# Short-convolution layer on one core: the weight sums of w_out made in the two-tile stage and kept in HBM, 15 seven-product pairs in place of 10

## The chip, the core and the metric

One NeuronCore of a Trainium2 chip. TensorE (PE) multiplies, with its weight loads (PEld) beside it; VectorE (DVE) and ScalarE (ACT) work on elements; GpSimd (POOL) does some adds and issues DMAs of its own; SyncE (SP) issues nearly all other DMAs. The metric is device time of one execution, in microseconds (us), median over runs; lower is better.

## What is computed

One layer of a decoder trunk for 256 tokens of width D = 2048, with E = 4096 channels, all in float32:

```python
h = rmsnorm(x, norm_g)
shift, scale, gate = split(silu(c) @ ada_w + ada_b, 3)
h = h * (1 + scale) + shift
b_gate, c_gate, v, g = split(h @ w_in, 4)          # w_in is D x 4E
u = causal_depthwise_conv(c_gate * v, conv_w)      # width 3
y = b_gate * u * silu(g)
x = x + gate * (y @ w_out)                         # w_out is E x D
return rmsnorm(x, final_g)
```

## The kernel before

Every float32 product is done as three products of reduced parts (`triple`): with a = a_hi + a_lo, the terms are hi*hi, hi*lo and lo*hi. So each weight tile is loaded by DMA, its high part is cast on ScalarE (line 380, and 842), and its low part, the difference, is made on VectorE (line 385, and 845). Weight tiles are 128 x 2048 (1 MB) in a pool `wpool` with three places of each kind, used in turn: "raw", "hi" and "lo".

The program has three stages. In the first (tiles `mm_s`) 16 of the 32 channel tiles are projected while the modulation is still being summed. In the **two-tile stage** (tiles `mm_b`, loop `for ct in range(NS, NCT, 2)`) the other 16 are projected two at a time: for each pair of channel tiles four quarters of w_in, and for each quarter two steps of one weight tile with 48 matmuls of 128x256. That makes 64 steps. After each step `gate_piece` adds a part of the sums for the gate: a load `at_g` and two multiply-adds on VectorE, 32 pieces in all, in four column groups. When a group is complete, GpSimd folds its 128 partitions in seven rounds (two copying DMAs into `turned` and an add each, lines 708 to 710), and adds it to the gate's bias (line 712), which SP has loaded onto all partitions (line 673).

In the **w_out stage** y is multiplied by w_out in two passes: first columns 0 to 1023, then 1024 to 2047 (of which the last 512 are partly done in a closing part with the channels in `LAST`). A pass (`columns`) goes over *pairs* of channel tiles in a written order; a pair is 256 rows of w_out. A plain pair needs eight triples, 24 matmuls of 128x512. A pair in `SEVEN` is done by a Strassen-Winograd scheme on 2x2 blocks with seven triples, 21 matmuls. It needs sums of the pair's four weight blocks b0 to b3, which `seven` makes on VectorE (lines 837, 843, 844), and sums of the tokens, made for each such pair in the two-tile stage by `token_forms` and kept in SBUF (`form`). Pairs 10 to 15 are of that kind in the first pass, 10 to 13 in the second, and a plain pair mostly stands between two of them.

In this stage "lo" places hold what is loaded or summed (`raw_o`, `sums_o`), "raw" places hold low parts and "hi" places high parts. A place is given out in turn, so a tile waits for the last reader of the tile three places earlier. Each engine runs its instructions in the order in which the program's scheduler wrote them; SP too, so a DMA whose place is not free holds up the ones behind it. The order on an engine is the scheduler's unless a manual dependency sets it, such as `last_low`, which keeps pairs in sequence on VectorE.

Of the kernel before, what the change touches and what calls it, by code (L numbers as in the profile page):

```python
# [8 lines left out]
F32 = mybir.dt.float32  # L9
# [108 lines left out]
def short_conv_layer(ctx: ExitStack, tc: tile.TileContext, x, c, norm_g, ada_w, ada_b, w_in, conv_w, w_out, final_g, out):  # L118
# [551 lines left out]
    gates = [slot([P, 2, 512], f"gate{j}") for j in range(2)]  # L670
    zs = [slot([P, 2, 2, T], f"z{j}") for j in range(2)]
    for j in range(2):
        nc.sync.dma_start(
            gates[j].rearrange("p a f -> p (a f)"),
            ada_b[0:1, 2 * D + j * 1024 : 2 * D + (j + 1) * 1024].partition_broadcast(P),
        )

    def gate(dc):
        return gates[dc // 2][:, dc % 2, :]
# [14 lines left out]
    def gate_sums(dc, j, at3):  # L694
# [10 lines left out]
        if j + 2 == KT:  # L705
# [6 lines left out]
            nc.gpsimd.tensor_tensor(out=gate(dc), in0=ga, in1=gate(dc), op=ALU.add)  # L712
# [3 lines left out]
    SEVEN = range(10, 16)  # L716
# [3 lines left out]
    def token_forms(pair, u):  # L720
# [9 lines left out]
        if pair < 14:  # L730
# [9 lines left out]
        nc.vector.tensor_tensor(out=lo, in0=sums, in1=hi.bitcast(F32), op=ALU.subtract)  # L740

    for ct in range(NS, NCT, 2):
        for q in QUARTERS:
            bank = psum.tile([P, CT, T], F32, tag="mm", name="mm_b")[:, 0:2]
            col = q * E + ct * P
            for kp in range(0, KT, KP):
# [12 lines left out]
                gate_piece()  # L759
            z = zs[q // 2][:, q % 2]  # L760
# [20 lines left out]
    W = 512  # L781
# [6 lines left out]
    def load_ends(n):  # L788

        if 0 <= n < TT:  # L790
            nc.sync.dma_start(xr[:, n, :], x[n * P : (n + 1) * P, :])
        elif n == TT:
            nc.sync.dma_start(fg, final_g.rearrange("(o d) -> o d", o=1).partition_broadcast(P))

# [6 lines left out]

    def load_o(raw, e0, ne, c0, n):
        nc.sync.dma_start(
            raw.rearrange("p (k f) -> p k f", k=ne),
            w_out[0, e0 * P : (e0 + ne) * P, c0 : c0 + n].rearrange("(k p) f -> p k f", p=P),
        )
# [9 lines left out]
    def residual(t, c0, n, src, pr):  # L816
# [3 lines left out]
        g = gates[c0 // 1024].rearrange("p a f -> p (a f)")[:, c0 % 1024 : c0 % 1024 + n]  # L820
        nc.vector.tensor_tensor(out=pr, in0=src, in1=g, op=ALU.mult)
# [9 lines left out]
    def seven(j, raw, bank, p1, p6, p75, opens, last):  # L831


        sums = w_tile("lo", "sums_o")
        hi, lo = hi_tile(), lo_tile("raw")
        b, s, bh, bl = (v.rearrange("p (b f) -> p b f", f=W) for v in (raw, sums, hi, lo))
        first = nc.vector.tensor_tensor(
            out=s[:, 0:2], in0=b[:, 1:3], in1=b[:, 0:1].to_broadcast([P, 2, W]), op=ALU.subtract
        )
        if last_low[0] is not None:  # L840
            tc.add_manual_dep(first.ins, last_low[0].ins.name, after, reason="the pair in front comes first")
        nc.scalar.copy(bh[:, 1:4], b[:, 1:4])
# [178 lines left out]
```

## Time and profile before

| | |
|---|---|
| median of 3 runs | 901.03 us (900.9 to 901.96) |
| span of the profiled execution | 898.9 us |
| what lies around the span, from the median | 2.1 us |
| VectorE busy in the span | 75% |
| ScalarE busy in the span | 54% |
| DMA moved | 235.53 MB, mean 262 GB/s |

The span is the time from the first to the last instruction of one execution. The page gives the busy share of each engine, the chain of work that ended last (followed back from the last instruction to what released each), the groups of instructions with their mean duration, the idle time in front of them and what ended it, and the DMA issues with the time to landing. A row of windows gives for each stretch the busy us of PE, PEld, DVE, ACT and POOL with their instruction counts, then the granted clock, the busy share of the DMA engines and GB/s.

### The profile page before, as it was taken

Reading aid. Unit: us, or ns where it says so; the run is one execution under the profiler, and the core shown is the slowest. Engines: PE = TensorE matmul, PEld = TensorE weight load, DVE = VectorE, ACT = ScalarE, POOL = GpSimd, SP = SyncE. Lnnn points to the kernel's source line nnn. Section 1 sums busy time; section 2 is a strip of 40 time slices with the busy share of each in tenths; the row PEclk is TensorE's granted clock in tenths of the full one; section 3 lists DMA queues with packets and bytes.
Section 4 is the critical chain, followed back from the end, with each engine's and each line's share of the span. In section 5 each row is a group of like instructions: output and inputs, shape, how many; then the busy total and the mean of one; then the engine's idle time right before and its main releaser. Section 6 shows DMA issues by size and latency. Waiting matters only on the chain.

```text
span 898.9 us, 16428 instructions
## 1 busy us (share of the span) xinstructions
PE 886.5 (99%) x6989; PEld 849.7 (95%) x6989; DVE 674.4 (75%) x667; ACT 484.0 (54%) x430; POOL 95.6 (11%) x107
## 2 busy tenths in 40 slices
PE   7999999999999999999999999999999999999996
PEld 4999999999999999999999999999999988888885
DVE  5899988899888866755965677565555578879896
ACT  6768866665558856644433444443434445554543
POOL 0000001010000134024134103410000000000000
PEclk9999999999999999999999999999999999999998
DMA  9999999999998597687888789766666476674662
GB/s 309 369 369 368 369 336 361 347 365 367 372 318 291 167 277 231 196 266 244 278 246 242 252 273 274 233 207 204 193 188 188 141 290 224 192 276 126 202 234 94
DMA packets 160250, 235.53 MB, mean 262 GB/s; under 512 B 7028, under 2 KB 105924, under 8 KB 159792
## 3 DMA queue, kind: packets, MB, share of 16 engines
q1 hardware_dynamic: 156368, 226.52, 76.8%
q0 software_dynamic: 3680, 7.92, 3.2%
q8 instruction: 55, 0.90, 0.4%
q14 instruction: 19, 0.16, 0.0%
q10 hardware_dynamic: 128, 0.04, 0.0%
HBM read 224.49 MB, written 2.10 MB: 252 GB/s over the span
## 4 chain that ended last, share of the span: by engine, by line
PE 97%; DMA 2%; SPq 0%; ACT 0%; issue 0%; ACTq 0%; DVE 0%
PE mm_s L545 39%; PE mm_b L545 39%; PE mm_w L814 7%; PE mm_o L814 7%; PE mm L814 4%; DMA at<-in_ada_w_dram 2%; PE sum L418 0%; SPq L240 0%; PE tp_g L530 0%; PE tp_g L526 0%; ACT big L928 0%; ACTq L1017 0%; ACT fs L918 0%; ACT z L991 0%; DVE fs L919 0%
## 5 line engine op out<-in xcount | busy, mean ns | idle before, releaser
L545 PE MATMUL mm_b<-hT,hi 128*128 128x256 f32 x2048 | 348.2, 276 | 0.0
L545 PE MATMUL mm_s<-hT,hi 128*128 128x256 f32 x2048 | 335.6, 277 | 0.0
L545 PEld LDWEIGHTS mm_b<-hT,hi 128*128 128x128 f32 x2048 | 308.1, 188 | 0.0
L545 PEld LDWEIGHTS mm_s<-hT,hi 128*128 128x128 f32 x2048 | 299.0, 188 | 0.2
L545 PE MATMUL mm_b<-hT,lo 128*128 128x256 f32 x1024 | 282.6, 276 | 0.0
L545 PE MATMUL mm_s<-hT,lo 128*128 128x256 f32 x1024 | 261.3, 276 | 0.0
L385 DVE TENSOR_TENSOR lo<-raw,hi 128x2048 fp32r<-128x2048 f32 (+1 forms) x66 | 152.4, 2311 | 103.1 <-ACT hi L380 102.6
L380 ACT CAST hi<-raw 128x2048 fp32r<-128x2048 f32 (+1 forms) x66 | 123.7, 1874 | 192.7 <-PE mm_b L545 146.6
L545 PEld LDWEIGHTS mm_b<-hT,lo 128*128 128x128 f32 x1024 | 192.2, 188 | 0.0
L545 PEld LDWEIGHTS mm_s<-hT,lo 128*128 128x128 f32 x1024 | 182.4, 188 | 0.0
L385 DVE TENSOR_TENSOR lo<-raw_s,hi 128x2048 fp32r<-128x2048 f32 (+1 forms) x80 | 149.1, 1871 | 34.7 <-ACT hi L380 34.2
L380 ACT CAST hi<-raw_s 128x2048 fp32r<-128x2048 f32 (+2 forms) x81 | 124.1, 1541 | 61.7 <-PE mm_s L545 46.7
L515 DVE SCALAR_TENSOR_TENSOR gv<-at,silu_c,gv 128x512 f32<-128x512 f32 x105 | 79.0, 752 | 5.5 <-DMA at<-in_ada_w_dram 3.6
L568 ACT COPY acc<-mm_s 128x1024 f32<-128x1024 f32 x54 | 54.6, 1012 | 37.0 <-PE mm_s L545 37.0
L385 DVE TENSOR_TENSOR lo<-raw_o,hi 128x2048 fp32r<-128x2048 f32 x22 | 50.4, 2290 | 22.9 <-ACT hi L380 22.9
L380 ACT CAST hi<-raw_o 128x2048 fp32r<-128x2048 f32 x22 | 42.0, 1908 | 45.8 <-DMA raw_o<-in_sc_w_out_dram 12.3
L814 PE MATMUL mm_w<-hi,y 128*128 128x512 f32 x184 | 58.8, 389 | 0.0
L710 POOL TENSOR_TENSOR gacc<-gacc,z 128x512 f32<-128x512 f32 x28 | 45.6, 1628 | 106.8 <-DMA z<-gacc 106.8
L814 PE MATMUL mm_o<-hi,y 128*128 128x512 f32 x176 | 55.3, 389 | 0.0
L704 DVE SCALAR_TENSOR_TENSOR gacc<-at_g,silu_c,gacc 128x512 f32<-128x512 f32 x60 | 46.9, 782 | 6.0 <-DMA at_g<-in_ada_w_dram 4.8
L814 PEld LDWEIGHTS mm_w<-hi,y 128*128 128x128 f32 x184 | 34.5, 188 | 7.2
L582 ACT COPY mm_s<-acc 128x1024 f32<-128x1024 f32 x38 | 38.6, 1017 | 2.6 <-DVE acc L571 1.8
(161 smaller groups left out, 670.8 us busy)
## 6 DMA issues: line engine op xcount, KB each, us to landing
raw<-in_sc_w_in_dram SPq DMA_DIRECT2D x64, 1024.0 KB, 5.8
raw_s<-in_sc_w_in_dram SPq DMA_DIRECT2D x47, 1024.0 KB, 7.9
raw_o<-in_sc_w_out_dram SPq DMA_DIRECT2D x32, 1024.0 KB, 5.2
at<-in_ada_w_dram SPq DMA_DIRECT2D x126, 256.0 KB, 7.8
raw_s<-in_sc_w_in_dram SPq DMA_DIRECT2D x33, 512.0 KB, 7.3
at_g<-in_ada_w_dram SPq DMA_DIRECT2D x32, 512.0 KB, 8.0
x<-in_x_dram SPq DMA_DIRECT2D x4, 512.0 KB, 6.2
big<-in_x_dram SPq DMA_DIRECT2D x2, 1024.0 KB, 8.2
```

The lines of the kernel that those rows point to most:

```text
L380: nc.scalar.copy(hi[:, :n], raw[:, :n])
L385: last_low[0] = nc.vector.tensor_tensor(out=lo[:, :n], in0=raw[:, :n], in1=hi[:, :n].bitcast(F32), op=ALU.subtract)
L515: nc.vector.scalar_tensor_tensor(out=gv, in0=at4[:, i], scalar=c_k, in1=gv, op0=ALU.mult, op1=ALU.add)
L545: mm = last_mm[0] = nc.tensor.matmul(dst, w, h[k], start=begins and left, stop=ends, skip_group_check=True)
L568: nc.scalar.copy(acc[ch, q], bank)
L582: nc.scalar.copy(bank, acc[ch, q])
L704: nc.vector.scalar_tensor_tensor(out=ga, in0=at3[:, i, :], scalar=s, in1=ga, op0=ALU.mult, op1=ALU.add)
L710: nc.gpsimd.tensor_tensor(out=ga, in0=ga, in1=turned, op=ALU.add)
L814: nc.tensor.matmul(dst, y[a], b, start=opens and i == 0, stop=ends and i == 2, skip_group_check=True)
```

## The change

The block sums of the weights are no longer made in `seven`. A new `weight_sums` runs after each step of the two-tile stage; at 15 of the 64 steps (4, 8, ... 60) it loads the pair's 1 MB of w_out into a "raw" place, makes the sums on VectorE in a "lo" place, and GpSimd stores them to HBM (`made`). In the w_out stage `seven` loads the ready sums into a "lo" place, and only three of the pair's four blocks (two DMAs). Pairs 8 to 15 use seven products in the first pass and 9 to 15 in the second, in new orders. The forms of pairs 8 and 9 need room: they take the two places that held the gate, which now waits as one row in HBM. The row begins as the bias, each folded group is added to it by an accumulating DMA, and SP loads it onto all partitions in the w_out stage, once the forms in those places have been used.

```diff
-    gates = [slot([P, 2, 512], f"gate{j}") for j in range(2)]
+    gate_slots = [slot([P, 2, 4, P], f"gate{j}", F32R) for j in range(2)]
...
-    for j in range(2):
-        nc.sync.dma_start(
-            gates[j].rearrange("p a f -> p (a f)"),
-            ada_b[0:1, 2 * D + j * 1024 : 2 * D + (j + 1) * 1024].partition_broadcast(P),
-        )
+    gate_row = dram.tile([1, D], F32, tag="gate_row", name="gate_row")
+    nc.gpsimd.dma_start(gate_row, ada_b[0:1, 2 * D : 3 * D])
...
+    def load_gate(j):
+
+        c0 = j * 1024
+        nc.sync.dma_start(gate_columns(c0, 1024), gate_row[0:1, c0 : c0 + 1024].partition_broadcast(P))
...
-            nc.gpsimd.tensor_tensor(out=gate(dc), in0=ga, in1=gate(dc), op=ALU.add)
+            nc.gpsimd.dma_start(gate_row[0:1, dc * 512 : (dc + 1) * 512], ga[0:1], accum_op=ALU.add)
...
-    SEVEN = range(10, 16)
+    W = 512
+    SEVEN = range(8, 16)
+    SEVEN_2 = range(9, 16)
...
+    UNITS = [(0, j) for j in SEVEN] + [(2 * W, j) for j in SEVEN_2]
+    SUMS_AT = {4 + 4 * i: unit for i, unit in enumerate(UNITS)}
...
+        raw, sums = raw_tile("raw_u"), w_tile("lo", "sums_u")
+        load_o(raw, 2 * j, 2, c0, 2 * W)
+        b, s = (v.rearrange("p (b f) -> p b f", f=W) for v in (raw, sums))
+        nc.vector.tensor_tensor(out=s[:, 0:2], in0=b[:, 1:3], in1=b[:, 0:1].to_broadcast([P, 2, W]), op=ALU.subtract)
+        nc.vector.tensor_tensor(out=s[:, 2], in0=b[:, 2], in1=s[:, 0], op=ALU.add)
+        nc.vector.tensor_tensor(out=s[:, 3], in0=b[:, 3], in1=s[:, 2], op=ALU.subtract)
+        made[unit] = dram.tile([P, SLOT], F32, tag=f"sums{c0}_{j}", name="made")
+        nc.gpsimd.dma_start(made[unit], sums)
...
                 gate_piece()
+                weight_sums()
...
         elif n == TT:
             nc.sync.dma_start(fg, final_g.rearrange("(o d) -> o d", o=1).partition_broadcast(P))
+        elif n == 6:
+            load_gate(0)
...
         sums = w_tile("lo", "sums_o")
+        nc.sync.dma_start(sums, made[c0, j])
         hi, lo = hi_tile(), lo_tile("raw")
...
-        first = nc.vector.tensor_tensor(
-            out=s[:, 0:2], in0=b[:, 1:3], in1=b[:, 0:1].to_broadcast([P, 2, W]), op=ALU.subtract
-        )
...
-        nc.vector.tensor_tensor(out=s[:, 2], in0=b[:, 2], in1=s[:, 0], op=ALU.add)
-        all_sums = nc.vector.tensor_tensor(out=s[:, 3], in0=b[:, 3], in1=s[:, 2], op=ALU.subtract)
...
-            load_o(raw, 2 * j, 2, c0, 2 * W)
+            if j in sevens:
+                blocks = raw.rearrange("p (b f) -> p b f", f=W)
+                e = 2 * j * P
+                nc.sync.dma_start(blocks[:, 1], w_out[0, e : e + P, c0 + W : c0 + 2 * W])
+                nc.sync.dma_start(blocks[:, 2:4].rearrange("p b f -> p (b f)"), w_out[0, e + P : e + 2 * P, c0 : c0 + 2 * W])
+            else:
+                load_o(raw, 2 * j, 2, c0, 2 * W)
...
-        0, (0, 1, 10, 2, 11, 3, 12, 4, 13, 5, 14, 6, 15, 7, 8, 9), SEVEN,
+        0, (0, 1, 8, 2, 9, 10, 3, 11, 12, 4, 13, 14, 15, 5, 6, 7), SEVEN,
...
-    LAST = (3, 4)
+    LAST = (2, 3)
...
-        2 * W, (0, 1, 2, 10, 3, 11, 4, 12, 5, 13, 14, 15), SEVEN[0:4],
-        lambda t, d: halves[d][:, t], *po, p75, False,
+        2 * W, (0, 1, 9, 10, 11, 2, 12, 13, 14, 15, 3, 8), SEVEN_2,
+        lambda t, d: halves[d][:, t], *po, p75, False, lambda n: load_gate(1) if n == 5 else None,
```

How the written order moves, at three places. First SP's queue at the start of the w_out stage, before: the raw tiles of pairs 10, 2, 11 and 3 around the loads of x and final_g (`big`).

```order
L803 DMA raw_o_8411<-in_sc_w_out_dram 128x2x1024
L803 DMA raw_o_8446<-in_sc_w_out_dram 128x2x1024
L791 DMA big_8341<-in_x_dram 128x2048 x2
L793 DMA big_8341<-in_final_g_dram 128x2048
L803 DMA raw_o_8476<-in_sc_w_out_dram 128x2x1024
L803 DMA raw_o_8512<-in_sc_w_out_dram 128x2x1024
```

The same place now: raw 8 (two DMAs), raw 2, x, the sums of 8, final_g, raw 9, raw 10, the sums of 9, the gate's first half, the sums of 10.

```order
L908 DMA raw_o_8545<-in_sc_w_out_dram 128x1024
L776 DMA raw_o_8579<-in_sc_w_out_dram 128x2x1024
L830 DMA big_8475<-in_x_dram 128x2048 x2
L869 DMA sums_o_8548<-made_4796 128x2048
L832 DMA big_8475<-in_final_g_dram 128x2048
L907 DMA raw_o_8609<-in_sc_w_out_dram 128x512
L908 DMA raw_o_8609<-in_sc_w_out_dram 128x1024
L907 DMA raw_o_8644<-in_sc_w_out_dram 128x512
L908 DMA raw_o_8644<-in_sc_w_out_dram 128x1024
L869 DMA sums_o_8613<-made_5072 128x2048
L686 DMA gate0_4480<-gate_row_4486 128x1024
L869 DMA sums_o_8648<-made_5322 128x2048
```

The sums of a pair are now loads in SP's queue, behind x for pair 8, and the gate's load stands between two of them.

ScalarE's casts at the same place, before: pair 1, raw 10, two small casts, the sums of 10, pair 2, raw 11.

```order
L380 CAST hi_8383<-raw_o_8381 128x2048
L842 CAST hi_8414<-raw_o_8411 128x1536
L480 CAST y15_4479<-z1_4483 128x2x256
L380 CAST hi_8421<-sums_o_8413 128x2048
L739 CAST form_h_8338<-z0_4482 128x512
L380 CAST hi_8448<-raw_o_8446 128x2048
L842 CAST hi_8480<-raw_o_8476 128x1536
```

And now: pair 1, raw 8, the small casts, pair 2, the sums of 8, raw 9, raw 10, the sums of 9.

```order
L380 CAST hi_8517<-raw_o_8515 128x2048
L872 CAST hi_8550<-raw_o_8545 128x1536
L480 CAST y15_4479<-z1_4483 128x2x256
L751 CAST form_h_8472<-z0_4482 128x512
L380 CAST hi_8581<-raw_o_8579 128x2048
L380 CAST hi_8554<-sums_o_8548 128x2048
L872 CAST hi_8615<-raw_o_8609 128x1536
L872 CAST hi_8650<-raw_o_8644 128x1536
L380 CAST hi_8619<-sums_o_8613 128x2048
```

The cast of a pair's sums has moved behind the cast of the pair after it (pair 2 ahead of the sums of 8, raw 10 ahead of the sums of 9).

Third, GpSimd in the two-tile stage, in the fold of the first column group of the gate; before, rounds follow each other without anything between them. Now the stores of the sums stand between rounds:

```order
L716 DMA z0_4482<-gacc_4545 16x512
L773 DMA made_4796<-sums_u_4791 128x2048
L717 TENSOR_TENSOR gacc_4545<-gacc_4545,z0_4482 128x512
L715 DMA z0_4482<-gacc_4545 120x512
L716 DMA z0_4482<-gacc_4545 8x512
L717 TENSOR_TENSOR gacc_4545<-gacc_4545,z0_4482 128x512
```

A store waits for VectorE's sums, and the rounds behind it on GpSimd wait with it; before, this queue held only the folds.

More of the change, by code (lines that the diff above doesn't have):

```diff
@@ L729, in token_forms @@
         nc.vector.tensor_tensor(out=s4, in0=a12, in1=s2, op=ALU.subtract)
-        if pair < 14:
+        if pair < 10:
+            form = gate_slots[pair - 8]
+            hi, lo = form[:, 0], form[:, 1]
+        elif pair < 14:
             form = adap.tile([P, ASLOT], F32R, tag="at", name="form", bufs=4).rearrange("p (h s f) -> p h s f", h=2, f=P)
@@ L778, in short_conv_layer @@
         gate_piece()
-    W = 512
     big = hpool.tile([P, 3 * D + W], F32, tag="big", name="big")
@@ L878, in columns @@
             if j in sevens:
-                seven(j, raw, bank, p1, p6, p75, j == sevens[0], j == sevens[-1])
+                seven(j, c0, raw, bank, p1, p6, p75, j == sevens[0], j == sevens[-1])
                 if j == sevens[-1]:
```

38 lines of the change are left out of this document (24 added, 14 removed).

## The prediction

> **What bounds the kernel now.** I read the page from the top (busy time, chain), then the chain in order of time, then the groups and the DMA answers of the stage that the change rebuilds.
>
> ```profile
> span 898.9 us, 16428 instructions
> PE 886.5 (99%) x6989; PEld 849.7 (95%) x6989; DVE 674.4 (75%) x667; ACT 484.0 (54%) x430; POOL 95.6 (11%) x107
> PE 97%; DMA 2%; SPq 0%; ACT 0%; issue 0%; ACTq 0%; DVE 0%
> ...
> 375.88 348.16 PE mm_b L545 x3072
> 724.04 10.89 PE mm_w L814 x48
> ```
>
> TensorE is the bound: the chain is its matmuls for 97% of the span. The two-tile stage runs from 375.88 for 348.16 us, 64 steps of 48 matmuls, so 5.44 us a step. The w_out stage begins at 724.04, and 48 of its 128x512 matmuls take 10.89 us, 0.2269 us each. A plain pair (24) takes 5.45 us, a seven-product pair (21) 4.76 us. Whatever leaves TensorE shortens the span as long as weights are ready in time. That condition needs the rows that feed it:
>
> ```profile
> L380 ACT CAST hi<-raw_o 128x2048 fp32r<-128x2048 f32 x22 | 42.0, 1908 | 45.8 <-DMA raw_o<-in_sc_w_out_dram 12.3 <-PE mm_w L814 12.1 <-DVE raw_o L964 8.6
> L842 ACT CAST hi<-raw_o 128x1536 fp32r<-128x1536 f32 x10 | 14.8, 1480 | 19.1 <-DMA raw_o<-in_sc_w_out_dram 10.1 <-PE mm_o L814 5.3 <-PE mm_b L545 3.7
> L385 DVE TENSOR_TENSOR lo<-raw_o,hi 128x2048 fp32r<-128x2048 f32 x22 | 50.4, 2290 | 22.9 <-ACT hi L380 22.9
> L845 DVE TENSOR_TENSOR lo<-raw_o,hi 128x1536 fp32r<-128x1536 f32 x10 | 17.5, 1750 | 0.0
> L837 DVE TENSOR_TENSOR sums_o<-raw_o 128x1024 f32<-128x1024 f32 x10 | 12.2, 1219 | 0.0
> L844 DVE TENSOR_TENSOR sums_o<-raw_o,sums_o 128x512 f32<-128x512 f32 x10 | 6.9, 691 | 0.3
> L843 DVE TENSOR_TENSOR sums_o<-raw_o,sums_o 128x512 f32<-128x512 f32 x10 | 6.9, 690 | 0.3
> DMA to landing us min/median/max: 4.9/5.2/7.9
> ```
>
> The last line is of the raw_o tile. ScalarE already waits for loads (12.3 and 10.1 us), yet TensorE does not: there is little slack. Each weight tile passes load, cast on ScalarE, low part on VectorE, and only then is its place free. There are three "lo" places. How fast a load can be:
>
> ```profile
> raw_o<-in_sc_w_out_dram SPq DMA_DIRECT2D x10, 1024.0 KB, 5.1
> ...
> raw_o<-in_sc_w_out_dram SPq DMA_DIRECT2D x2, 1024.0 KB, 5.3
> big<-in_x_dram SPq DMA_DIRECT2D x2, 1024.0 KB, 8.2
> big<-in_final_g_dram SPq DMA_DIRECT2D x1, 1024.0 KB, 11.2
> 722.78 0.37 SPq L803 DMA_DIRECT2D raw_o<-in_sc_w_out_dram  x1
> 723.39 0.82 SPq L791 DMA_DIRECT2D big<-in_x_dram  x2
> 724.25 0.73 SPq L793 DMA_DIRECT2D big<-in_final_g_dram  x1
> 728.00:736.00 8.00, 8.00 (x37) 6.64 (x36) 5.07 (x5) 3.41 (x3) 0.00 (x0) 1.00 1.01 424
> ```
>
> The first row is of 740 to 790, where loads mostly run alone; the rest is of the stage's start. Four 1 MB loads are queued between 722.78 and 724.25; the first lands at 728.1, the last at 724.25 + 11.2 = 735.4. So behind each other they take 2.45 us each, and the window 728 to 736 moves 424 GB/s. A lone one took 5.1 (I use 5.05): 2.6 fixed and 2.45 of transfer.
>
> **The change, part by part.** The profiled execution is the span, 898.9; the median of the runs is 901.03, and I carry the 2.1 us around the span over unchanged.
>
> 1. *Products.* Five more seven-product pairs: 15 x 0.2269 = **-3.4 us**, all on TensorE.
>
> 2. *VectorE in w_out* loses 1.22 + 0.69 + 0.69 = 2.6 us for each of the ten old pairs. It is not waited for by TensorE now, so this alone is worth nothing; what is late next is the load, because the sums now come from HBM and hold a "lo" place while they load.
>
> 3. *The ring of three places.* A full tile holds a place for 5.05 + 1.91 + 2.29 = 9.25 us; the three-block raw tile of a seven-product pair (two DMAs, 0.75 MB, by the same two terms about 4.6) for 4.6 + 1.48 + 1.75 = 7.8. A seven-product pair needs both: 17.1 / 3 places = 5.7 us, against 4.76 us on TensorE. Before, its sums needed no load, and a plain pair stood between any two until the last ones. Now there are runs of two, three and four. So TensorE must wait where a run outlasts what is prepared. I carried this rule tile by tile through the written order: a load starts when the tile three places earlier has its low part and SP has come to it; loads queue at 2.45 us per MB; a cast waits for landing, for ScalarE's order and for TensorE's release of the "hi" place. To test the rule, I ran it over the old order: no wait of TensorE, and the cast of pair 12's raw tile at 748.5; the trace has
>
> ```profile
> 748.60 1.48 ACT L842 CAST hi<-raw_o 128x1536 fp32r<-128x1536 f32 x1 [1.28 <-DMA raw_o<-in_sc_w_out_dram]
> ```
>
> For the new order (times as if w_out begins at 724.04; pair 8 starts at 734.93):
>
> - *Sums of pair 8*: their place comes free at 724.04, SP has issued both loads of x ahead, so they land at 735.3; ScalarE's order has pair 2 first, which waits for pair 1's end: casts 734.95 to 736.85, then 738.75. TensorE wants them after 10 products, at 737.2: waits 1.6.
> - *Sums of pair 9*: place free when the sums of pair 8 have their low part (741.4), landed 746.5; ScalarE does raw 10 first (place free at 746.7): 748.2, cast done 750.1, low part 752.4; wanted 749.2, and the low part three products on: waits 0.9 + 1.6.
> - *Raw 3*: has that place, free at 752.4, landed 757.5, cast 759.4, low 761.7; wanted 28 products after 752.4, at 758.8: waits 0.7, with raw 11 (cast 760.9) 1.0, low part 0.6.
> - Sums of 15 and raw 5 at the end of the first pass: 0.5 + 0.3.
> - *Second pass, sums of pair 11*: the residual's VectorE work delays raw 10's low part to 827.3; SP then stands at the gate's load until pair 9 is done with that place (828.1), so landed 834.4, cast 836.3, low 838.6; wanted 835.4: waits 0.9 + 1.6.
> - Raw 14 0.3, sums of 15 1.5 (low part at 864.95, wanted 863.4), raw 3 0.9.
>
> Sum: 7.2 + 5.3 = **+12.5 us**. With 2.2 us per MB instead of 2.45 it is 11, with 2.8 it is 15. Bounds: 0, if every load is hidden, and 17, if the whole deficit 5.7 - 4.76 of 15 pairs is paid and the late start's 3 us with it. I take 12.5.
>
> The Trainium skill speaks of this rate: "DMA: Bandwidth & Descriptors", Specifications, gives about 358 GB/s of HBM per core and a vendor's derate of 368 GB/s. By 368, a 1 MB load takes 2.85 us, and the rule gives 16 us of waits and about 915.6; the measured 424 GB/s in the window above speaks against it, so the row's 2.45 stands.
>
> 4. *Two-tile stage.* Fifteen units of 1 MB load, 2.6 us of VectorE and 1 MB store by GpSimd, one per four steps.
>
> ```profile
> raw<-in_sc_w_in_dram SPq DMA_DIRECT2D x64, 1024.0 KB, 5.8
> 540.00:560.00 20.00, 20.00 (x179) 20.00 (x179) 17.18 (x16) 8.25 (x7) 7.30 (x8) 1.00 0.96 285
> 600.00:700.00 100.00, 100.00 (x885) 100.00 (x884) 54.07 (x45) 41.61 (x32) 0.00 (x0) 1.00 0.64 196
> POOL gacc L710 <- DMA z<-gacc: 106.8, 28, 7.6
> ```
>
> From 600 on VectorE is busy 54% and the DMA engines 64%: 2.6 us in 21.75 and 2 MB more (96 GB/s) fit, price nothing. In the gate's stretch they do not: at 540 to 560 VectorE's 17.18 of 20 becomes 19.6, and DMA at 0.96 gets a third more to move. The sums also take a "lo" place in turn, so the next low part starts when a step begins and not a step earlier: 5.44 - 2.29 = 3.1 us of slack are left there. I take one overrun of **+2 us**, at the last gate sums. The store has no row: a place goes back when it lands, and the low part three steps on needs it 16.5 us after the sums are made (four steps, less some 3 us until the sums are done and 2.3 for the low part); GpSimd may first stand 7.6 us in the gate's fold. Below 8.9 us of landing it costs nothing. Nearest rows: 5.05 for a lone load as large, 8.3 median for raw loads from 380 to 400, their worst stretch:
>
> ```profile
> raw<-in_sc_w_in_dram SPq DMA_DIRECT2D x4, 1024.0 KB, 8.3
> ```
>
> So bounds 0 (5.05 is hidden; the waiting VectorE has no work to gain) and +9 (ten units beside the fold, each 0.9 late).
> "DMA: Bandwidth & Descriptors", Anatomy of one DMA (the Trainium skill), fits a GpSimd-issued DMA as 2.0 us + bytes/436e3: an estimate of 4.4 us for 1 MB; by it the store costs nothing. No row of before shows it.
>
> 5. *Gate and forms.* The gate's wait for its bias row goes, with four adds; all are GpSimd's, which the chain never names:
>
> ```profile
> POOL gate L712 <- DMA gate<-in_ada_b_dram: 27.9, 1, 27.9
> ```
>
> Price 0. Its two half-megabyte loads move into w_out and are in the waits above. Two more token forms are short VectorE and ScalarE work in steps with room; 0, or 1 us if that room is gone.
>
> Sum: 901.0 - 3.4 + 12.5 + 2.0 = **912**.
>
> **Rivals.**
> *Everything is hidden (the other side).* If the head start of three prepared tiles carries every run, the time is 901.0 - 3.4 = 897.6. It decides at a place turn of 3 x 4.76 / 2 = 7.1 us on average per tile; rows give (9.25 + 7.8) / 2 = 8.5, and no load landed below 4.9. For it: the old order never let TensorE wait. Chance 0.08.
> *Only part of the waits.* If ScalarE's or SP's order hurts less than written (3 to 7 us of waits): 901 to 905. Chance 0.09, of which 0.03 is within 0.2% of before.
> *The store is slow, or the DMA engines overflow in the gate's stretch*, landing over 9 us: the forecast's 910 of w_out and products plus 9, about 919. For it: 0.96 busy there and raw loads at 8.3. Against: the folds' stretch ends, and raw loads land two steps early. Chance 0.18.
> *The change does not do what it says*: the order counts 723 against 738 of these matmuls, and no sums on VectorE in w_out; no chance.
>
> **How the numbers follow.** Forecast 0.65 (906 to 918, from w_out waits of 8 to 17 and 0 to 4 before). Predicted 912; the range 904 to 920 leaves out the hidden case, most of the partial one below it and the top of the slow store. What a measurement tells from no change is about 0.2%, 1.8 us. Slower 0.65 + 0.18 + 0.06 = 0.89, same 0.03, faster 0.08.
>
> **What would show it.** TensorE busy share falling in 735 to 765 and 830 to 870, with PE idle before hi and lo of sums tiles and of raw 3; ScalarE's casts of sums released by DMA; raw_o and sums loads landing at about 5; no PE wait from 600 to 720; the store landing under 9 us. It is wrong if sums loads land by 3.5, if written order is not what the engines meet, or if the two-tile stage waits more than w_out.

## The result, and the profile after

The changed kernel takes **949.46 us** (median of 5 runs, 947.6 to 951.21) against 901.03: 1.053 times as long, 95% interval 1.0515 to 1.0544. The prediction said slower, 912, and its range ended at 920. The profiled execution has a span of 945.9, 47.0 more than before; its run took 947.63.

The page of the changed kernel: span, busy time, shares of the chain.

```profile
span 945.9 us, 16596 instructions
PE 900.0 (95%) x6974; PEld 855.0 (90%) x6974; DVE 703.8 (74%) x697; ACT 493.1 (52%) x437; POOL 102.2 (11%) x123
PE 59%; DMA 18%; issue 10%; DVE 6%; ACT 4%; POOL 2%; SPq 0%; ACTq 0%; DVEq 0%; POOLq 0%
```

TensorE was 97% of the chain and is now 59%; transfers, VectorE, ScalarE and GpSimd have come in between. TensorE is also busy for 13.5 us longer, with 15 matmuls fewer. Where that lies is read from the two stages. The first pair of windows is of before, the second of the changed kernel (us of the stretch, busy us of PE, PEld, DVE, ACT, POOL, granted clock, share of the DMA engines, GB/s):

```profile
375.88:724.04 348.16, 348.16 (x3073) 348.16 (x3073) 218.44 (x191) 146.40 (x113) 60.89 (x67) 1.00 0.74 228
724.04:891.70 167.66, 167.64 (x738) 138.09 (x737) 142.22 (x116) 80.99 (x59) 0.00 (x0) 1.00 0.61 205
```

```profile
375.88:749.77 373.89, 357.09 (x3073) 355.63 (x3072) 264.38 (x246) 148.20 (x116) 82.58 (x95) 0.97 0.93 296
749.77:938.48 188.71, 172.12 (x724) 135.83 (x722) 126.28 (x90) 88.26 (x65) 0.00 (x0) 0.98 0.71 250
```

The two-tile stage is **25.7 us** longer, the w_out stage **21.0** in spite of the 15 matmuls saved. In each there are two parts. One is idle: 373.89 - 357.09 = 16.8 us and 188.71 - 172.12 = 16.6 us. The other is matmuls that take longer: the two-tile stage has as many as before and is busy 8.9 us more, and w_out, by its count, should be 3.4 us less busy than before and is 4.5 more, so 7.9. The clock column, 0.97 and 0.98 instead of 1.00, says what part of that is. By the spacing of the matmuls, some 7 of the 8.9 us and 2.8 of the 7.9 were lost at half clock; most of the rest is matmuls that come late right behind a wait, called refilling below.

What TensorE waited for, first in the two-tile stage, then in w_out, without its two smallest rows (us in total, times, longest):

```profile
PE mm_b L545 <- DVE lo L385: 15.5, 6, 5.1
PE mm_b L545 <- ACT hi L380: 1.3, 1, 1.3
```

```profile
PE mm L849 <- ACT hi L872: 5.2, 3, 2.7
PE mm L849 <- ACT hi L380: 4.7, 5, 1.7
PE mm L849 <- DVE lo L385: 4.4, 4, 1.4
PE mm_w L849 <- DVE lo L385: 1.5, 1, 1.5
```

The longest wait, 5.1 us, can be followed back through three engines. The timelines of GpSimd, VectorE and TensorE (start, us, engine, line, operation; in brackets the idle time before and what ended it; rows between these are left out):

```profile
314.37 0.51 POOL L716 DMA_DIRECT2D z<-gacc  x1
395.10 0.58 POOL L773 DMA_DIRECT2D made<-sums_u  x1 [80.22 <-DVE sums_u L771]
436.94 1.28 POOL L717 TENSOR_TENSOR gacc<-gacc,z 128x512 f32<-128x512 f32 x1 [6.62 <-DMA z<-gacc]
438.52 0.83 POOL L719 DMA_DIRECT2D gate_row<-gacc  x1 [0.30 <-POOL gacc L717]
```

```profile
440.96 0.49 DVE L709 TENSOR_SCALAR gacc<-at_g,silu_c 128x512 f32<-128x512 f32 x1 [9.84 <-DMA gate_row<-gacc]
442.94 3.35 DVE L385 TENSOR_TENSOR lo<-raw,hi 128x2048 fp32r<-128x2048 f32 x1
```

```profile
446.34 0.58 PE L545 MATMUL mm_b<-hT,lo 128*128 128x256 f32 x1 [5.06 <-DVE lo L385]
457.00 0.58 PE L545 MATMUL mm_b<-hT,lo 128*128 128x256 f32 x1 [3.16 <-DVE lo L385]
```

The first store reached the head of GpSimd's queue at 314.9, in the middle of the first fold, and stood there for 80 us, until VectorE had made the sums that it stores. The fold's other rounds stood behind it, and ended at 438. Before, nothing stood between the rounds, and the same fold ran from 309 to 362 (its first and last row):

```profile
308.92 0.55 POOL L708 DMA_DIRECT2D z<-gacc  x1 [77.42 <-DVE acc L626]
360.65 1.29 POOL L710 TENSOR_TENSOR gacc<-gacc,z 128x512 f32<-128x512 f32 x1 [2.88 <-DMA z<-gacc]
```

The third group of gate sums on VectorE reuses the place of the first: it waited 9.84 us, with low parts of weights behind it. TensorE waited for these.

After such a wait comes the second price. Windows of 2 us behind it:

```profile
446.00:448.00 2.00, 1.66 (x7) 1.66 (x8) 1.97 (x4) 0.00 (x0) 0.00 (x0) 0.50 0.37 106
448.00:450.00 2.00, 2.00 (x11) 2.00 (x11) 2.00 (x3) 0.00 (x0) 0.00 (x0) 0.50 0.92 259
450.00:452.00 2.00, 2.00 (x19) 2.00 (x19) 2.00 (x4) 0.00 (x0) 0.30 (x1) 0.98 0.99 333
```

TensorE works, but at a granted clock of 0.50: 11 matmuls in 2 us where there are 18 otherwise. The half clock lasts 3.7 us here, of which half is lost. The Trainium skill, "TensorE: Matmul & The Clock Gate", Part 1, describes this: half rate after an idle window, full rate again after about 3.4 us of work. The trace agrees with 3.7 us; how much idle time it takes here stands in the last section.

### The profile page after: what moved, and what is told of

Same layout as the page of the kernel before. It is cut to its first block, busy times and chain, and to the rows that moved or that the text cites. A ratio compares the mean times of both kernels' runs of the same rounds, so it can differ in the third digit from the quotient of the medians.

```text
span 945.9 us, 16596 instructions
## 1 busy us (share of the span) xinstructions
PE 900.0 (95%) x6974; PEld 855.0 (90%) x6974; DVE 703.8 (74%) x697; ACT 493.1 (52%) x437; POOL 102.2 (11%) x123
## 4 chain that ended last, share of the span: by engine, by line
PE 59%; DMA 18%; issue 10%; DVE 6%; ACT 4%; POOL 2%; SPq 0%; ACTq 0%; DVEq 0%; POOLq 0%
PE mm_s L545 29%; PE mm_b L545 19%; DMA raw<-in_sc_w_in_dram 6%; PE mm_w L849 5%; DMA z<-gacc 4%; PE mm_o L849 4%; DVE lo L385 3%; DMA raw_o<-in_sc_w_out_dram 3%; ACT hi L380 3%; PE mm L849 2%; DMA at<-in_ada_w_dram 2%; DMA sums_o<-made 2%; POOL gacc L717 1%; DMA raw_u<-in_sc_w_out_dram 1%; DVE gacc L711 1%
## 5 line engine op out<-in xcount | busy, mean ns | idle before, releaser
L545 PE MATMUL mm_b<-hT,hi 128*128 128x256 f32 x2048 | 355.0, 279 | 1.3 <-ACT hi L380 1.3
L545 PEld LDWEIGHTS mm_b<-hT,hi 128*128 128x128 f32 x2048 | 313.5, 191 | 1.5 <-ACT hi L380 1.5
L545 PE MATMUL mm_b<-hT,lo 128*128 128x256 f32 x1024 | 286.7, 280 | 15.5 <-DVE lo L385 15.5
L545 PEld LDWEIGHTS mm_b<-hT,lo 128*128 128x128 f32 x1024 | 195.5, 191 | 16.7 <-DVE lo L385 16.6
L385 DVE TENSOR_TENSOR lo<-raw_o,hi 128x2048 fp32r<-128x2048 f32 x17 | 38.9, 2291 | 24.0 <-ACT hi L380 24.0
L385 DVE TENSOR_TENSOR lo<-sums_o,hi 128x2048 fp32r<-128x2048 f32 x15 | 34.4, 2292 | 29.9 <-ACT hi L380 29.9
L849 PE MATMUL mm_w<-hi,y 128*128 128x512 f32 x160 | 53.9, 402 | 0.5 <-ACT hi L380 0.5
L380 ACT CAST hi<-raw_o 128x2048 fp32r<-128x2048 f32 x17 | 32.4, 1907 | 38.6 <-DMA raw_o<-in_sc_w_out_dram 14.3
L849 PE MATMUL mm_o<-hi,y 128*128 128x512 f32 x140 | 45.1, 389 | 0.0
L380 ACT CAST hi<-sums_o 128x2048 fp32r<-128x2048 f32 x15 | 28.6, 1903 | 24.6 <-DMA sums_o<-made 19.1
```

The costliest lines, as they stand in the source:

```text
L380: nc.scalar.copy(hi[:, :n], raw[:, :n])
L385: last_low[0] = nc.vector.tensor_tensor(out=lo[:, :n], in0=raw[:, :n], in1=hi[:, :n].bitcast(F32), op=ALU.subtract)
L545: mm = last_mm[0] = nc.tensor.matmul(dst, w, h[k], start=begins and left, stop=ends, skip_group_check=True)
L849: nc.tensor.matmul(dst, y[a], b, start=opens and i == 0, stop=ends and i == 2, skip_group_check=True)
```

## The experiments

"Lost" means beyond the 348.2 us of the two-tile stage, or beyond 167.7 us of w_out less 0.2269 us for each matmul saved. A *unit* is one call of `weight_sums`: the load, the sums and the store of one pair. The *recurrence* is the prediction's rule, carried tile by tile through the written order. Runs e1 to e7, e9, e10 and e12 were executed once each; the runs of before beside them lay between 900.4 and 901.96. Seven runs of e8 spread over 8 us, so small differences are read from stages and waits, not from the time alone.

### The two-tile stage

**e1: the stores on another queue.**

```diff
-        nc.gpsimd.dma_start(made[unit], sums)
+        nc.scalar.dma_start(made[unit], sums)
```

> The changed kernel, with its fifteen stores issued by ScalarE's queue and not by GpSimd's; nothing else differs. Theory 1 (GpSimd's queue): the first store stood between two rounds of the first gate fold and held the fold, and so VectorE's next gate sum; without it the losses of TensorE at 441 to 460 go (gaps 5.1 and 3.2, with refilling and half clock 11.7 us in all) and the fold of the first piece of the gate runs through by about 350 to 361. The two-tile stage is then near 373.9 - 11.7 = 362 us, the time near 938. Theory 2 (DMA only): the loads are late because the engines are full, so the stage stays at 372 to 376 us and the time at 947 to 951.

932.73 us. The two-tile stage takes 362.0 us, and there is no wait before 468.

```profile
375.80:737.80 362.00, 353.41 (x3074) 351.63 (x3073) 259.30 (x248) 148.38 (x115) 50.03 (x58) 0.99 0.92 300
```

The 11.7 us of 441 to 460 are gone, as theory 1 had it; the fold runs from 304 to 357. What is left lies at 468 to 567, 13 us. Time was better than expected by 5; 3 of these are in w_out.

**e2: half of each unit's load left out.**

```diff
-        load_o(raw, 2 * j, 2, c0, 2 * W)
+        load_o(raw[:, : 2 * W], 2 * j, 1, c0, 2 * W)
...
```

> The changed kernel, but each unit loads only half of its weights (0.5 MB, the first contraction block) and makes its sums of them, with the same VectorE operations and the same 1 MB store; the output leaves the other block's part of the sums out. Theory 2 (DMA): with 7.5 MB less to move, loads land earlier and the losses of TensorE at 530 to 585 (13.1 us with refilling and half clock) shrink to 0 to 4; those at 441 to 460 stay: time 936 to 941. Theory 1 alone (the store's place in GpSimd's queue sets everything): no change, 947 to 951.

959.82 us, longer than the changed kernel, which neither theory had. The scheduler wrote another order with it. The fold ends at 433, sooner than in the changed kernel, but on VectorE the gate sum that waits for it now stands ahead of two low parts that the changed kernel makes first. It waits 11.1 us, and the longest wait of TensorE is 9.8 us, at 431 to 441:

```profile
DVE gacc L709 <- DMA gate_row<-gacc: 11.1, 1, 11.1
```

The edit also takes only 0.5 MB a unit away, 24 GB/s. It tells neither theory from the other.

**e6: as e1, with 64 KB instead of 512 KB for each piece of the gate.**

```diff
-        nc.sync.dma_start(at3, adas[:, j : j + 2, 2, dc * 512 : (dc + 1) * 512])
+        nc.sync.dma_start(at3[:, 0, 0:P], adas[:, j, 2, dc * 512 : dc * 512 + P])
+        part = at3[:, 0, 0:P].unsqueeze(1).to_broadcast([P, 4, P])
...
```

> As e1 (stores by ScalarE's queue, all fifteen units from step 4 on), but each piece of the gate loads 64 KB instead of 512 KB; VectorE's gate sums and GpSimd's folds have the same number and sizes. The output leaves most of the gate's weights out. Theory B (weights 193, gate 96 and units 96 GB/s are together more than the DMA engines move, and the loads are late): the losses at 468 to 567 of e1 (13.2 us) shrink to 0 to 2, the two-tile stage is 348 to 350 us and the time 919 to 922. Rival (VectorE's work or the lo places set them): two-tile stage still near 362, time 931 to 934.

923.37 us, the stage 350.3.

```profile
375.80:726.10 350.30, 348.81 (x3074) 348.42 (x3073) 261.15 (x248) 148.25 (x115) 47.46 (x55) 1.00 0.91 294
```

Median landing times (the last number, us) of the loads of weights, of the units' loads and of the stores in the stretch from 460 to 570, first in before, then in e1, then in e6:

```profile
raw<-in_sc_w_in_dram SPq DMA_DIRECT2D x20, 1024.0 KB, 6.3
```

```profile
raw<-in_sc_w_in_dram SPq DMA_DIRECT2D x19, 1024.0 KB, 9.3
made<-sums_u ACTq DMA_DIRECT2D x5, 1024.0 KB, 8.4
raw_u<-in_sc_w_out_dram SPq DMA_DIRECT2D x5, 1024.0 KB, 8.7
```

```profile
raw<-in_sc_w_in_dram SPq DMA_DIRECT2D x20, 1024.0 KB, 7.7
made<-sums_u ACTq DMA_DIRECT2D x5, 1024.0 KB, 6.9
raw_u<-in_sc_w_out_dram SPq DMA_DIRECT2D x5, 1024.0 KB, 7.1
```

And the same stretch as a window, in before, e1 and e6:

```profile
460.00:570.00 110.00, 110.00 (x973) 110.00 (x973) 73.68 (x65) 44.94 (x34) 29.25 (x31) 1.00 0.84 258
```

```profile
460.00:570.00 110.00, 101.41 (x860) 99.63 (x859) 83.26 (x84) 41.60 (x32) 18.84 (x24) 0.98 0.98 323
```

```profile
460.00:570.00 110.00, 109.50 (x966) 109.30 (x966) 87.59 (x85) 44.86 (x35) 25.27 (x29) 1.00 0.97 312
```

With smaller loads of the gate these transfers land some 1.5 us sooner and TensorE waits 0.5 us instead of 8.6, while VectorE does more (87.6 us against 83.3). So VectorE's work is ruled out, and late landing holds. The sum in the expectation was wrong, though: the gate's eight pieces of this stretch do not come one a step at 96 GB/s but within 35 us (514 to 547 in e1). Over the whole stretch the share of the DMA engines hardly differs, 0.98 and 0.97; from 514 to 547 it is 1.06 in e1 and 0.93 in e6. Of the 25.7 us, 11.9 went with the stores' queue and 11.7 more with the gate's loads; 2.1 remain.

**e12, e13, e15: the queue alone.** Fifteen stores of 4 KB at the units' steps, without a unit's load, sums or place; w_out as in e3.

```diff
+        sums = const.tile([P, 8], F32, tag="tiny", name="tiny", bufs=2)
+        first = nc.vector.tensor_copy(sums, silu_c[:, 0:8])
...
+        nc.gpsimd.dma_start(made[unit], sums)
```

> As e3 (loads in place of the sums in w_out), but with fifteen tiny stores in the two-tile stage at the units' steps: VectorE copies 128x8 behind that step's low part, and GpSimd stores the 4 KB. No unit's load, sums or lo place. The first store stands behind the second round of the first gate fold on GpSimd, the second behind its sixth, as one round later and just so in the changed kernel. Queue alone: the fold is held by about 80 us, VectorE's first gate sum of the third piece comes too late, TensorE loses near 11.7 us at 440 to 460 and the time is 933 to 936. Queue and slow rounds together: held to about 392, the fold still has five rounds; at the 6.5 us of a round before, and not the 8 to 9 of the changed kernel, it ends by 428, before VectorE needs its place at 431: no wait, the time 923 to 926.

955.47 us, outside both: the matmuls of the first two stages were slower, from the start. Run again it was the same:

> The kernel of e12 once more, since all its matmuls of that run were 4% slower than in any other (172 in 20 us instead of 179), which hides its cost. Queue alone: TensorE loses near 11.7 us at 440 to 460, time 933 to 936. Queue and slow rounds together: the fold ends by 428, no wait there, time 923 to 926.

953.32 us (952.98 to 953.65). Neither showed a wait at 440 to 460, but at another pace of TensorE. In e15 the 64 bytes a partition of the new tiles are taken off an unused one, so that all others lie as before:

```diff
-    const.tile([P, 48], F32, tag="line0", name="line0")
+    const.tile([P, 32], F32, tag="line0", name="line0")
```

> The kernel of e12 and e13, with the 64 bytes a partition that its two small tiles added taken off the unused tile line0, so that all larger tiles lie where they do in the kernel before. If the shift of addresses made all matmuls 4% slower in e12 and e13, the spacing is back at 179 in 20 us; else it stays at 172. Then as before: queue alone, TensorE loses near 11.7 us at 440 to 460 and the time is 933 to 936; queue and slow rounds together, no wait there and 923 to 926.

932.49 us (931.75 and 933.23). A window of the first stage in e13, where nothing of the edit runs, and the same in e15:

```profile
340.00:360.00 20.00, 20.00 (x171) 20.00 (x170) 13.72 (x15) 13.33 (x14) 0.00 (x0) 1.00 0.66 211
```

```profile
340.00:360.00 20.00, 20.00 (x179) 20.00 (x178) 12.28 (x10) 11.83 (x12) 0.00 (x0) 1.00 0.60 189
```

The pace is back with the addresses. The fold is held for 77.7 us as in the changed kernel, but ends at 427 instead of 438; TensorE waits 2.6 us between 435 and 461, in five short waits without half clock, and 2.3 us more later; the stage takes 355.7. So neither expectation holds alone: the queue by itself costs 3.5 of the 11.7 us there, and 7.5 in the whole stage. The rest of the 11.7 comes with the units' bytes, sums and places. In the changed kernel the store went 4 us later (395 and not 391), and the five rounds behind it took 43 us and not 36; their copies landed after 6.9 us and not 4.7 (medians from 376 to 470). That full DMA engines alone make the rounds slow is argued, not shown.

**e5: seven units behind the gate's pieces** (steps 38 to 62), the other sums replaced by loads.

```diff
-    SUMS_AT = {4 + 4 * i: unit for i, unit in enumerate(UNITS)}
+    SUMS_AT = {38 + 4 * i: unit for i, unit in enumerate(UNITS[:7])}
```

> The changed kernel with seven units instead of fifteen, at steps 38, 42 ... 62 of the two-tile stage, behind the gate's pieces and folds; the other eight pairs load 1 MB of w_out where their sums should be, so the output leaves those sums out. Theory A (units cost only where they meet the gate's loads and folds): no wait of TensorE in the two-tile stage, which is back at 348 us; w_out's order comes out a little different, with 8.2 us of waits by the recurrence and 13 to 20 lost with refilling and half clock: time 911 to 918. Rival (each unit costs by itself, 25.5 / 15 = 1.7 us): two-tile stage 360, time 923 to 930.

929.78 us, the rival's time, but not by its mechanism. In the two-tile stage there is one wait, at 600, and six of the seven units cost nothing:

```profile
600.66 2.29 DVE L385 TENSOR_TENSOR lo<-raw,hi 128x2048 fp32r<-128x2048 f32 x1 [9.34 <-DMA made<-sums_u]
```

Here the first store stood on GpSimd behind the last rounds of a fold until 596, and its "lo" place was missing: the same queue in the other direction, 2.9 us of wait and 2.8 of half clock. w_out lost 25 us; the recurrence gave 8.2 us of waits for its order and 15.4 were measured, its worst miss, which is not explained.

### The w_out stage

**e3: no units; the sums' places are filled by loads of w_out.**

```diff
-                weight_sums()
...
-        nc.sync.dma_start(sums, made[c0, j])
+        load_o(sums, 2 * j, 2, c0, 2 * W)
```

> No units in the two-tile stage; the w_out stage is the changed one in order and places, but each load of sums brings 1 MB of w_out itself, so the output leaves the sums out. The two-tile stage should be back at 348.2 us. Theory 3 (ring of three places): w_out stays at 188 to 189 us, as in the changed kernel, so the time is near 901.0 + 21 = 922. Rival (what w_out lost comes from reading the stored sums, or from stores still in flight): w_out is 176 to 180 us as the recurrence gave it, the time 909 to 913.

923.84 us. Two-tile stage 348.2, w_out 191.0 against 188.7 in the changed kernel. The same stage took 185.6 in e1 and 188.0 in e6, so 191.0 is within what runs differ by: what w_out lost does not depend on the stores or on reading them.

**e9: the sums need no load and no place.**

```diff
-        sums = w_tile("lo", "sums_o")
-        nc.sync.dma_start(sums, made[c0, j])
+        sums = raw
...
```

As in e3 there are no units; each pair's own tile is loaded whole, 1 MB.

> As e3 (no units), with the changed order and all fifteen seven-product pairs, but the sums need neither a load nor a place: the pair's own weights are cast and split a second time as if they were the sums (ScalarE's and VectorE's casts and low parts are all there). The output leaves the sums out. Theory 3 (a load of sums that holds one of three places is what TensorE waits for): the recurrence gives no wait, w_out is 167.7 - 3.4 = 164.3 us and the time 897 to 899. Rival (ScalarE's order, VectorE or the start's loads of x make the waits): w_out stays above 172, the time above 905.

898.68 us, below every run of before (lowest 900.4). All waits of TensorE in w_out are in one row:

```profile
PE mm L848 <- ACT hi L870: 0.2, 1, 0.2
```

Same pairs, same casts, same low parts, same loads of x: without the fifteen loads into the ring, the 15.6 us of waits in e3 are one of 0.2. So VectorE's work, the casts themselves and the loads of x are not what TensorE waits for.

ScalarE's order is not the same, though. In e9 a pair's second cast stands right behind its first (raw 8, sums of 8, pair 2); in e3 and the changed kernel that of pairs 8 and 9 stands behind the next pair's first (raw 8, pair 2, sums of 8). So e9 shows that the loads make the waits together with the places and the order that come with them; it does not price these apart. In the changed kernel both are seen: the sums of 8 landed at 761.0 and were cast at 762.6, behind pair 2, but the sums of 10, raw 3 and raw 11 were cast within 0.1 us of landing (at 778.2, 783.6 and 787.5).

**e4: the ten pairs and orders of before, with loaded sums**, and **e7: fifteen pairs, alternating with plain ones.**

```diff
-        0, (0, 1, 8, 2, 9, 10, 3, 11, 12, 4, 13, 14, 15, 5, 6, 7), SEVEN,
+        0, (0, 1, 10, 2, 11, 3, 12, 4, 13, 5, 14, 6, 15, 7, 8, 9), range(10, 16),
...
```

```diff
-        0, (0, 1, 8, 2, 9, 10, 3, 11, 12, 4, 13, 14, 15, 5, 6, 7), SEVEN,
+        0, (0, 1, 8, 2, 9, 3, 10, 4, 11, 5, 12, 6, 13, 7, 14, 15), SEVEN,
...
```

The orders of the second pass, left out here, are changed in the same way, and `LAST` in e4.

> As e3, but with the ten seven-product pairs and the orders of the kernel before (a plain pair between any two of them until the last ones); each pair's sums are a 1 MB load. The output leaves the sums out. Theory 3 (runs of seven-product pairs outlast the ring): waits shrink to 4.4 us by the same recurrence, at the sums of the first, second and third pair, with refilling 5 to 8: time 906 to 909. Rival (each load of sums costs by itself, about 20 us / 15 = 1.4 us a pair): 10 x 1.4 = 14, time 915.

> As e3 (no units, loads in place of the sums), but fifteen seven-product pairs in an order with a plain pair between any two for as long as there are plain pairs; the rest of the run at the end of each pass. The output leaves the sums out. Rule of thumb (a plain and a seven-product pair take 10.2 us on TensorE, their three tiles (9.25 + 17.1) / 3 = 8.8 us of the ring): only the start and the ends wait, w_out 172 to 178 us, time 905 to 912. The recurrence: 16.2 us of waits, more than the 12.5 of the changed order, 2.7 at the start of the second pass and 6.5 in its last pieces; with refilling and half clock time 925 to 931.

e4: 919.21 us, of which w_out lost 10 (5.6 of waits, expected 4.4), between the two expectations. The other 8 are a side effect in the two-tile stage. No product uses the forms in the gate's places here, which is probably why the scheduler put the gate's load early in SP's queue. There it waited for a fold, with weight loads behind it:

```profile
SPq L686 <- DMA gate_row<-gacc: 20.6, 1, 20.6
```

e7: 925.47 us, 17.6 of waits where the recurrence gave 16.2; the rule of thumb falls. Alternating is no better than the runs of two to four, since what it gains in a pass it loses at the start of the second pass (4.9 in one wait) and at the end.

### The second price of a wait

**e10: before, with idle VectorE work ahead of some low parts.**

```diff
+        first = nc.vector.memset(idle, 0.0)
+        for _ in range(n):
+            last = nc.vector.tensor_tensor(out=idle, in0=idle, in1=idle, op=ALU.add)
```

> The kernel before with idle VectorE work (6 to 15 additions of 128x512 on zeros, 0.69 us each) put ahead of a low part at steps 42, 45 ... 60 of the two-tile stage, where nothing else is late; its result is not changed. TensorE waits 0 to some 7 us each time. Theory C (a wait has a second price: after idle of more than about 2 us TensorE is granted half its clock for about 3.3 us, which is 1.6 us more lost, and about 0.17 us for refilling after any wait): gaps under 1.8 us are followed by full speed, those over 2.3 by 14 to 18 matmuls at twice the spacing, though the DMA engines are at 0.6 here. Rival (the slow matmuls after the waits come from the full DMA engines of that stretch): full speed after all gaps.

908.12 us. The low parts were further ahead than thought, so that only the longest delays made a wait: 1.7 and 1.8 us with three matmuls between.

```profile
694.00:696.00 2.00, 0.45 (x2) 0.24 (x2) 2.00 (x1) 0.00 (x0) 0.00 (x0) 0.74 0.00 0
696.00:698.00 2.00, 1.73 (x8) 1.73 (x9) 1.97 (x4) 0.00 (x0) 0.00 (x0) 0.50 0.19 52
698.00:700.00 2.00, 2.00 (x11) 2.00 (x11) 1.94 (x2) 0.00 (x0) 0.00 (x0) 0.50 0.97 291
```

Half clock follows, at a DMA share of 0.00 ahead of it: it comes from the idle time, not from full DMA engines. Both waits are shorter than the 2.3 us from which theory C has half clock, so its limits do not hold as they stand. One event is all that this run gives; the last section reads all runs together.

### Towards a version that is faster

e9 is the ceiling for fifteen pairs, 2.8 us under before. Three kernels tried to reach some of it: before's pairs and two more, five stored sums, placed in w_out where the recurrence gave 0.3 us of waits. They differ in the units' steps alone.

```diff
+    SUMS_AT = dict(zip([38, 43, 48, 53, 58], STORED))  # e8
+    SUMS_AT = dict(zip([45, 49, 53, 57, 61], STORED))  # e11
+    SUMS_AT = dict(zip([40, 44, 48, 52, 56], STORED))  # e14
```

> Twelve seven-product pairs: those of the kernel before and pairs 8 and 9 of the first pass. Five of them (8, 9, 12, 13 of the first pass, 10 of the second) have stored sums, made by units at steps 38, 43, 48, 53 and 58 and stored by GpSimd; the other seven make them on VectorE in w_out, as before. The recurrence gives 0.3 us of waits against 1.4 us of products saved (6 x 0.2269): 900.0 to 900.5, within what can be told from before, or just faster. Rival (a unit or a stored sum costs by itself 1 to 2 us): 905 to 910.

> As e8, with the five units at steps 45, 49, 53, 57 and 61, well behind the last fold of the gate. Theory 1 again (in e8 the first store stood behind the fold's last rounds on GpSimd and held a lo place, in some runs long enough for a wait and half clock): the runs gather at 902 to 904, without the 908 to 911 of e8. Rival (the spread comes from w_out or from the stores themselves): the same spread from 903 to 911.

> As e8 and e11, with the five units at steps 40, 44, 48, 52 and 56: behind the gate's last fold as in e11, but at the same step of each group of four as the units of the changed kernel, where VectorE makes all the sums one behind the other. In e11 the last sum stood behind a convolution step that waited for ScalarE, so raw and lo places were held longer. Theory D (the step within the group decides): no wait of TensorE in the two-tile stage, w_out 168 to 170 us as in e8's profile, time 902 to 904, all runs within 1 us or so. Rival (1 MB stores by GpSimd hold lo places too long wherever they stand): waits of 3 to 8 us between 600 and 720, time 907 to 916.

e8: 908.14 us (902.78 to 911.04), ratio 1.0066 (1.0042 to 1.009). e11: 915.72 (914.25 to 916.24), 1.0152 (1.0135 to 1.0169). e14: 905.05 (903.35 to 906.23), **1.0038** (1.0024 to 1.0052). None is faster than before. In the profiles of e8 and e14 the two-tile stage has no wait and w_out takes 170.2, against 166.3 with no wait: 2.1 to 2.3 us of waits where 0.3 were expected, and 1.7 of refilling. e11 is slower than both of its expectations. Its w_out took 175.4, and in the two-tile stage TensorE waited 4.6 us; VectorE's timeline shows where from:

```profile
663.96 0.69 DVE L770 TENSOR_TENSOR sums_u<-raw_u,sums_u 128x512 f32<-128x512 f32 x1
668.20 0.89 DVE L472 SCALAR_TENSOR_TENSOR z<-z,cw,z 128x255 f32<-128x255 f32 x2 [3.55 <-ACT z L471]
669.00 0.69 DVE L771 TENSOR_TENSOR sums_u<-raw_u,sums_u 128x512 f32<-128x512 f32 x1
```

The last sum stands behind a convolution step that waits for ScalarE, and holds a raw and a lo place meanwhile. With the steps of e14 the sums follow each other, and the waits are gone: theory D holds for the two-tile stage, though the runs spread over 3 us where one was expected. Why single runs of e8 took 908 to 911 stays open, since the profiled one did not.

## Why the prediction was wrong, point by point

It is 37.5 us short. In the profiled run 23.7 of it lie in the two-tile stage and 11.9 in w_out; that run was 1.8 us below the median.

1. *Products, -3.4.* Right: 723 matmuls, and e9 shows the gain when nothing waits.

2. *VectorE in w_out, worth nothing alone.* Right: nothing came of it, and the load of the sums is what is late.

3. *The ring, +12.5.* The mechanism and the places were right. Moved by the 25.7 us that the stage begins later, the waits for the sums of pairs 8 and 9 were forecast at 764.5, 775.8 and 778.1, of 1.6, 0.9 and 1.6 us, and that for raw 11 at 786.6, of 1.0. The timeline has

```profile
764.50 0.73 PE L849 MATMUL mm<-hi,gate 128*128 128x512 f32 x2 [1.30 <-ACT hi L380]
776.14 0.74 PE L849 MATMUL mm<-hi,gate 128*128 128x512 f32 x2 [0.92 <-ACT hi L380]
778.47 0.50 PE L849 MATMUL mm<-lo,gate 128*128 128x512 f32 x1 [1.35 <-DVE lo L385]
789.08 0.80 PE L849 MATMUL mm<-hi,y 128*128 128x512 f32 x1 [2.75 <-ACT hi L872]
```

The term was mis-sized twice. Waits are 16.6 and not 12.5, near the upper bound of 17. The largest miss is the last row, raw 11: its loads were issued between those of raw 3 and of the sums of 11, and landed 7.4 us later. Loads that overlap landed later than 2.45 us per MB had them; the median of the sums' loads was 6.9 us (the first row below; the second is of the stores), where 5.05 was used for a free queue. And each wait was priced at its length. Behind a wait the first two matmuls come some 0.17 and 0.11 us late, and after the 2.75 us in the last row matmuls ran at half clock until 795, which lost 2.8 us: with a few shorter pauses, 7.9 us. The term measured 24.4.

```profile
sums_o<-made SPq DMA_DIRECT2D x15, 1024.0 KB, 6.9
made<-sums_u POOLq DMA_DIRECT2D x15, 1024.0 KB, 9.4
```

4. *Two-tile stage, +2 with bounds 0 and +9.* This is the step that failed; it was 25.7. "GpSimd may first stand 7.6 us in the gate's fold" looked at the store behind the fold, and never at the fold behind the store. Yet the order that the change section quotes has the store between two rounds, and the wait could be read beforehand: in the profile of before the fold began at 308.9, and the two-tile stage, in which the sums are made, at 375.9 (the first sums were there at 395). That cost 11.9 us (e1). The second half was read and not added up. "DMA at 0.96 gets a third more to move" was left at one overrun of 2 us. By the window of before that is quoted above, 460 to 570 has a share of 0.84 at 258 GB/s; with the units' 96 it is 0.84 x 354 / 258 = 1.15, more than there is, for 110 us. e6 shows 11.7 us for it; the last 2.1 of the 25.7 stay open. The rule is rough: for e6, where the gate's loads bring 33 GB/s less, it gives 1.04, and TensorE waited only 0.5 us. The Trainium skill's rule that was weighed ("DMA: Bandwidth & Descriptors", Specifications, 368 GB/s) would not have found this, since 354 is less. The traces show the engines full at 323 GB/s in e1 (share 0.98), at 355 in the first stage of before (the window below, share 1.04) and at 424 in the window that the prediction quotes (1.01), so the share tells more than the rate.

```profile
0.00:100.00 100.00, 94.83 (x747) 87.58 (x748) 81.92 (x110) 75.63 (x91) 1.38 (x7) 1.00 1.04 355
```

That from 600 on the units cost nothing was right: no wait there.

5. *Gate and forms, 0.* Right as far as it shows: no wait of TensorE names them. The landing of the gate's row is in the chain only because of the store ahead of the fold; 2.7 of VectorE's 9.84 us lie between the end of the last round, 438.2, and that landing.

The rival "the store is slow, or the DMA engines overflow" had the right stage and half of the cause (stores landed after 9.4 us in the median) but was priced by its places alone, 9 us.

## What to carry to other kernels

A DMA that waits, put on a queue that other work shares, is priced in both directions: what stands ahead of it, and what stands behind it until its data exist, with the time read from the profile of before. Where a stream is added, scale the DMA share of that stretch by the bytes; well above 1, loads land late and every ring that they fill turns more slowly. And a wait of TensorE costs more than its length: some 0.3 us of refilling each time and, where idle time adds up to about 1.8 us within 3.4 us, half clock, which costs half of the next 3 to 6 us of work.

## What the runs showed of the hardware that was not expected

Two small tiles that moved the others by 64 bytes in each partition made the 128x256 matmuls of the first two stages 4% slower (171 instead of 179 in 20 us, both at a granted clock of 1.00): e13 against e15. From start to start they took 118 ns instead of 113. The 128x512 matmuls of w_out took 230 instead of 227, so they hardly changed. The whole was 21 to 23 us longer, 14.6 of them in the first stage. In the two-tile stage it was 8.8, since at that pace the waits of e15 (4.9 us) were 0.3. An edit that adds a small tile can hide its own effect in this way. What addresses cost this is not known from these runs.

For single waits half clock had no sharp limit: a wait of 2.4 us in e1 was followed by full clock, one of 1.6 us in e4 by half clock. The limit is sharp when the traces are cut as the clock is. In each of the 17 traces the changes of the granted clock lie whole multiples of 3.41 us apart, and within the program half clock lasts one, two or three such windows. From 300 us on, all 30 windows at full clock in which TensorE idled 1.83 us or more were followed by half clock, and so were 8 of 13 with 1.59 to 1.82 us; none of some 2950 with less was. A window at half clock was followed by full clock where TensorE idled up to 0.54 us in it, and by another at half clock from 0.70 us on. The 2.4 us of e1 fell into two windows, 0.88 and 1.54 us; the two waits of e10 put 2.19 us into one. The page of the Trainium skill named above ("TensorE: Matmul & The Clock Gate", Part 1) asks for an idle window of about 3.4 us; the length of the window agrees, but here about half of it idle was enough.
